# A decoder trunk on one core: the down projection as seven products over quadrants, with their sums made during the up projection, and three moves in the front

## The chip, the core and the metric

The kernel runs on one core of a Trainium2 chip. Five engines have instruction streams of their own: TensorE (PE in the profile) multiplies matrices into eight banks of PSUM, VectorE (DVE) and GpSimd (POOL) do elementwise work, ScalarE (ACT) does casts, copies and activations, and SyncE (SP) does little else than issue DMAs. An engine takes its instructions in order; engines wait for each other by semaphores. SP's, ACT's and POOL's DMA issues stand in the same in-order streams.

The metric is the device time of one execution in microseconds (us). A profiled execution also gives a span, from the first to the last instruction.

## What is computed

```python
h = rmsnorm(x, norm_mix_g)                    # x: 1024 tokens x 1024 features
z = h @ w_in                                  # a_h a_b a_c | q k v | c_val c_gate
y_a = a_b * causal_dwconv(a_c * a_h, conv_a_w)
y_b = dilated_mixture(q, k, v, rel_bias)      # 8 heads of 64
u = causal_dwconv(c_val * sigmoid(c_gate), conv_c_w) + conv_c_b
y_c = silu(layernorm(u, ln_c_g, ln_c_b))
y = concat(rmsnorm(y_a), rmsnorm(y_b), rmsnorm(y_c))
x = x + y @ w_out
h = rmsnorm(x, norm_ffn_g)
gate, val = split(causal_dwconv(h @ w_up, conv_f_w))   # 2 x 2816
x = x + (silu(gate) * val) @ w_down           # 2816 x 1024
return rmsnorm(x, final_g)
```

All is float32. The inner dimension of the down projection is 2816, which is 22 feature steps of 128.

## The kernel before

**Arithmetic.** PE works on a rounded format (fp32r). To keep the precision of float32, every operand is cut into a high part (a cast on ACT, helper line L71) and a low part (a subtraction on DVE or POOL, line L72), and every product is made of three matmuls (`mm3`, lines L90 to L92): high by high, and the two of high by low. A matmul here has a 128x128 stationary and a 128x512 moving operand.

**Order.** The order of PE's instructions is the order of the code. The other engines' and the DMA queues' instructions are put in order by a scheduler, which places each where its own model of the run finds it ready; so an instruction can come to stand ahead of one that is written earlier. Tiles come from pools with few buffers, and a tile that is used again makes its next writer wait for its last reader.

**Front (to 445 us).** The input projections come first. While they run, DVE makes the 31-tap convolution of the third part, `conv_rest`, whose two halves are added to `ln_a` (L432). Column sums for the norms are made on PE (`st_ps`, L116) at set places of a later projection: a hook is called after so many of its steps, by the table `HK`; a second hook fetches the result (`st_c` on DVE, `tr_ps` on PE). q and k for a pair of heads are projected (`proj_qk`), split, stored to DRAM, and read back by head as `sa`, `sb` and `sm` (`load_head`, POOL's queue). Attention starts at 231 us (`s_ps`, L527), and between its steps PE does fill work from a generator: the remaining q and k, then `out_ac`, the output projection of two of the three parts, which needs `w_out` as `wac_hi` and `wac_lo`.

**Up projection (529 to 929 us).** The 1024x1024 products of a step j (one gate and one value tile of 128 features) are made as seven products on quadrants. `main(j)` runs 22 times: POOL makes four sums of weights (L971 to L974), operands are split, PE fills banks `cb`, and DVE adds them up (L979, L983, L988, L997, L1000) into `ut`. A three-tap convolution follows (`conv3`, ACT and four DVE operations at L960), then silu, and the product of gate and value (L1006), which is stored to DRAM as `actd[j]` (L1007), 128 features by 1024 tokens. `lead` makes the first two of the seven products ahead of time; steps 6, 13, 20 and 21 have none, and are shorter.

**Down projection (929 to 1173 us).** For each half of the tokens, PE goes over 22 feature steps; a step takes a 128x1024 tile of `w_down` and a 128x512 tile of `actd` from DRAM, splits them, and adds to eight banks. The first two steps of the first half have tiles loaded and split during the up loop (`early_tiles`, into buffers of the up projection). A bank that is done is added to x (L1098), squared and summed (ACT), and `finish` scales and stores the output.

## Time and profile before

| | us |
|---|---|
| median of three runs | 1182.11 (1181.99 to 1182.67) |
| profiled run | 1181.71 |
| its span | 1179.9 |
| PE busy | 1138.5 (96%) |
| DVE busy | 757.4 (64%) |
| POOL busy | 521.3 (44%) |
| ACT busy | 503.7 (43%) |

The mean granted clock of PE is 0.984 of full speed. In the rows below, times are in us from the start of the span unless marked ns. A timeline row gives start and length of an instruction (or of several of one kind, x4), engine, code line, operation, output <- inputs, and in brackets how long the engine was idle before and what released it. The length of a matmul is the life of one instruction in a pipeline and not the distance to the next. "PE f_ps L90 <- ACT wac_hi L71" reads: the matmul at L90 that writes f_ps waited for the cast that writes wac_hi. In a row of windows each engine's busy time is followed by its count of instructions; PEclk is the granted clock, and the last two numbers are the busy share of the DMA engines and GB/s.

### The profile page before, as it was taken

Reading aid. Unit: us, or ns where it says so; the run is one execution under the profiler, and the core shown is the slowest. Engines: PE = TensorE matmul, PEld = TensorE weight load, DVE = VectorE, ACT = ScalarE, POOL = GpSimd, SP = SyncE. Lnnn points to the kernel's source line nnn. Section 1 sums busy time; section 2 is a strip of 40 time slices with the busy share of each in tenths; the row PEclk is TensorE's granted clock in tenths of the full one; section 3 lists DMA queues with packets and bytes.
Section 4 is the critical chain, followed back from the end, with each engine's and each line's share of the span. In section 5 each row is a group of like instructions: output and inputs, shape, how many; then the busy total and the mean of one; then the engine's idle time right before and its main releaser. Section 6 shows DMA issues by size and latency. Waiting matters only on the chain.

```text
span 1179.9 us, 14291 instructions
## 1 busy us (share of the span) xinstructions
PE 1138.5 (96%) x5327; PEld 943.7 (80%) x5327; DVE 757.4 (64%) x886; ACT 503.7 (43%) x798; POOL 521.3 (44%) x328
## 2 busy tenths in 40 slices
PE   9999979899979999989999999999999999999997
PEld 7888868788858887868888888888887788888886
DVE  7599965356656666796677887788778722164214
ACT  7212115256555655573444444444444432343323
POOL 4223522423222203036677777777776043334331
PEclk9999989999989999989999999999999999999999
DMA  6218214977689604223242342332423554456531
GB/s 239 86 40 234 73 53 121 309 195 166 156 236 228 143 1 161 96 102 124 78 138 89 108 141 83 133 108 90 142 89 126 169 191 158 146 188 217 171 116 72
DMA packets 59317, 162.80 MB, mean 138 GB/s; under 512 B 6232, under 2 KB 15952, under 8 KB 59248
## 3 DMA queue, kind: packets, MB, share of 16 engines
q1 hardware_dynamic: 44784, 139.27, 36.1%
q0 software_dynamic: 12160, 16.78, 7.2%
q10 hardware_dynamic: 2304, 5.83, 1.4%
q8 instruction: 42, 0.69, 0.3%
q14 instruction: 27, 0.22, 0.1%
HBM read 127.17 MB, written 34.69 MB: 137 GB/s over the span
## 4 chain that ended last, share of the span: by engine, by line
PE 83%; DVE 6%; DMA 5%; ACT 3%; issue 2%; POOL 1%; SPq 0%; ACTq 0%; DVEq 0%; POOLq 0%
PE cb L91 8%; PE cb L90 8%; PE cb L92 8%; PE d_ps L92 7%; PE d_ps L91 6%; PE d_ps L90 6%; PE ca L92 4%; PE ca L90 4%; PE ca L91 4%; PE pv_ps L581 2%; PE f_ps L90 2%; PE f_ps L92 2%; PE f_ps L91 2%; PE t_ps L550 2%; PE v L92 1%
## 5 line engine op out<-in xcount | busy, mean ns | idle before, releaser
L72 POOL TENSOR_TENSOR w_lo<-w_raw,w_hi 128x1024 fp32r<-128x1024 f32 (+2 forms) x49 | 108.7, 2220 | 204.6 <-ACT w_hi L71 204.6
L960 DVE SCALAR_TENSOR_TENSOR x<-ut,pr,x 128x1024 f32<-128x1024 f32 x88 | 147.0, 1688 | 18.8 <-ACT x L958 18.0
L72 POOL TENSOR_TENSOR wd_lo<-w_raw,wd_hi 128x1024 fp32r<-128x1024 f32 x32 | 78.4, 2454 | 163.3 <-ACT wd_hi L71 150.7
L92 PE MATMUL d_ps<-wd_hi,a_lo 128*128 128x512 f32 x336 | 131.7, 392 | 1.2 <-DVE a_lo L72 1.2
L90 PE MATMUL d_ps<-wd_hi,a_hi 128*128 128x512 f32 x336 | 131.5, 391 | 0.5 <-ACT a_hi L71 0.5
L91 PE MATMUL d_ps<-wd_lo,a_hi 128*128 128x512 f32 x336 | 131.4, 391 | 0.5 <-POOL wd_lo L72 0.5
L72 DVE TENSOR_TENSOR a_lo<-a_raw,a_hi 128x512 fp32r<-128x512 f32 x42 | 40.0, 961 | 132.4 <-ACT a_hi L71 125.3
L71 ACT CAST w_hi<-w_raw 128x512 fp32r<-128x512 f32 (+2 forms) x61 | 46.1, 764 | 138.8 <-PE v L92 23.6
L298 DVE SCALAR_TENSOR_TENSOR yc<-u,pr,yc 128x1024 f32<-128x1024 f32 x60 | 89.7, 1548 | 1.7 <-ACT yc L295 1.4
L92 PEld LDWEIGHTS d_ps<-wd_hi,a_lo 128*128 128x128 f32 x336 | 63.5, 189 | 14.6 <-DVE a_lo L72 1.5
L90 PEld LDWEIGHTS d_ps<-wd_hi,a_hi 128*128 128x128 f32 x336 | 63.5, 189 | 14.2 <-ACT a_hi L71 1.0
L91 PEld LDWEIGHTS d_ps<-wd_lo,a_hi 128*128 128x128 f32 x336 | 63.4, 189 | 13.9 <-POOL wd_lo L72 0.8
L71 ACT CAST a_hi<-a_raw 128x512 fp32r<-128x512 f32 x42 | 25.8, 620 | 111.9 <-PE d_ps L91 108.6
L958 ACT ACTIVATE x<-ut,pr 128x1024 f32<-128x1024 f32 x44 | 50.7, 1153 | 47.8 <-DVE ut L1000 32.6
L537 ACT ACTIVATE p<-p,mn 128x128 f32<-128x128 f32 (+3 forms) x64 | 49.8, 778 | 40.5 <-DVE mn L534 40.3
L1006 DVE TENSOR_TENSOR x<-x 128x1024 f32<-128x1024 f32 x22 | 46.3, 2105 | 10.6 <-ACT x L1005 10.6
L71 ACT CAST wd_hi<-w_raw 128x1024 fp32r<-128x1024 f32 x42 | 43.9, 1048 | 20.0 <-DMA w_raw<-in 20.0
L997 DVE TENSOR_TENSOR ut<-cb,yb 128x512 f32<-128x512 f32 x22 | 15.2, 690 | 56.3 <-PE cb L92 56.3
L561 DVE TENSOR_TENSOR ptl<-t_ps,pth 128x512 fp32r<-128x512 f32 x48 | 33.1, 690 | 20.6 <-ACT pth L560 20.1
L971 POOL TENSOR_TENSOR xp<-xp 128x512 f32<-128x512 f32 x11 | 21.2, 1925 | 55.2 <-DMA xp<-in 49.8
L550 PE MATMUL t_ps<-ident,p 128*128 128x128 f32 x288 | 44.4, 272 | 0.0
L534 DVE CUSTOM_DVE_ANT_0 p<-l_ps,g 128x640 f32<-128x640 f32 (+5 forms) x34 | 33.8, 995 | 15.0 <-PE l_ps L528 14.4
(405 smaller groups left out, 3319.1 us busy)
## 6 DMA issues: line engine op xcount, KB each, us to landing
w_raw<-in SPq DMA_DIRECT2D x93, 512.0 KB, 3.7
ur<-in SPq DMA_DIRECT2D x22, 512.0 KB, 3.7
xp<-in SPq DMA_DIRECT2D x22, 512.0 KB
actd<-x SPq DMA_DIRECT2D x22, 512.0 KB
a_raw<-actd SPq DMA_DIRECT2D x42, 256.0 KB, 2.8
vd<-vt SPq DMA_DIRECT2D x8, 512.0 KB
vv<-vd POOLq DMA_DIRECT2D x8, 512.0 KB, 5.4
g<-fs SPq DMA_DIRECT2D x8, 512.0 KB, 9.5
```

The lines of the kernel that those rows point to most:

```text
L71: cp = A.copy(hi, src)
L72: lo_eng.tensor_tensor(out=lo, in0=src, in1=f(hi), op=ALU.subtract)
L90: T.matmul(ps, whi, xhi, start=start, stop=False, **kw)
L91: T.matmul(ps, whi, xlo, start=False, stop=False, **kw)
L92: T.matmul(ps, wlo, xhi, start=False, stop=stop, **kw)
L298: V.scalar_tensor_tensor(out=yc[i], in0=u[i][:, j:j + S], scalar=col("cwc", j * 2 + i), in1=yc[i], op0=ALU.mult, op1=ALU.add)
L534: V.tensor_tensor_reduce(out=p[:, :n], in0=ps[:, :n], in1=gq, op0=ALU.add, op1=ALU.min, scale=1.0, scalar=3e38, accum_out=mn[:, ix:ix + 1])
L537: mark["exp"] = A.activation(out=p[:, :n], in_=p[:, :n], func=AF.Exp, scale=-1.0, bias=mn[:, ix:ix + 1], accum_out=den[h // 2][:, dc:dc + 1])
L550: T.transpose(out=tp[:, i * P:(i + 1) * P], in_=p[:, kj * P:(kj + 1) * P], identity=ident)
L958: A.activation(out=c, in_=t[:, 2:], func=AF.Copy, scale=col("cwf", 2 * 44 + m))
L960: V.scalar_tensor_tensor(out=c, in0=t[:, q:q + S], scalar=col("cwf", q * 44 + m), in1=c, op0=ALU.mult, op1=ALU.add)
L1006: V.tensor_tensor(out=cg, in0=cg, in1=cv, op=ALU.mult)
```

## The change

**Down projection.** It becomes seven products over quadrants, as the up projection is. The activation (2816 x 1024 tokens) is cut into A11, A21 (features of steps 0 to 10, first and second half of the tokens) and A12, A22 (steps 11 to 21), and `w_down` into B11, B12 (steps 0 to 10, first and second half of the output columns) and B21, B22 (steps 11 to 21). P1 is A11 B11, P2 is A12 B21, and five more products work on the sums S1, S2 (of the activation) and T1, T2, T3 (of the weights) too. Each product goes over eleven feature steps with four banks, one for each 128 tokens; there are two sets of four banks, d_x and d_y, and P2 and P3 add on to what P1 and P5 left. A step loads each operand as a quadrant of 128x512, and P7, P4 and P3 load a third quadrant and subtract it on POOL.

T1 and T2 are made during steps 0 to 10 of the up loop, S1 and S2 during steps 11 to 21, one DVE and one POOL operation a step: `sums_load(j)` reads into the buffers that the product of gate and value leaves free, `sums_add(j)` adds and stores the sums to DRAM. T3 is made during P1, P6 and P2 (`third`). The early tiles now cover four feature steps of P1. The three matmuls in a bank and step stay as they were.

**Front.** The table `HK` gets other places, q and k of the first pair of heads stay in SBUF, and their loads are issued ahead of the last projection; `out_ac` loads the first half of `w_out` into other buffers before it opens its own, splits it in two cuts, and loads x on SP's queue.

```diff
-    HK = (6, 8, 8, 10, 9, 11, 5, 9)
+    HK = (10, 14, 7, 11, 8, 12, 5, 9)
...
         split(t[:, :S], hi, lo, G if tmp else V)
+        if i % 4 == 0:
+            qk[i] = hi, lo
+            return
         nc.sync.dma_start(out=qk[i][0], in_=f(hi))
...
     do_norm()
+    heads = {0: load_head(0), 1: load_head(1)}
     table(AF.Exp, "sqrt")
     proj_qk(5, 10, (yb[2], yb[3].bitcast(F32R), yb[2].bitcast(F32R)))
...
-        mark["w"] = split(raw, hi, lo, G)
+        for q in range(2):
+            q = slice(q * 512, q * 512 + 512)
+            mark["w"] = split(raw[:, q], hi[:, q], lo[:, q], G)
...
     def out_ac():
 
+        w2 = [wp_pair() for _ in range(2)]
+        for q, r in enumerate((0, 6)):
+            load_half(r, 0, *w2[q])
         close(c_x)
...
+            if dh == 0:
                 for q in range(2):
-                    load_row(2 + q, *wac[q])
+                    nc.sync.dma_start(out=xp2[q], in_=x_n[q * P:(q + 1) * P, :])
+                for q, r in enumerate((0, 6)):
+                    load_half(r, 1, *wac[q])
...
+    def sums_load(j):
+
+        cg, cv = xp2[2 * (j % 2)], xp2[2 * (j % 2) + 1]
+        if j < HF:
+            nc.sync.dma_start(out=cv, in_=w_down[j * P:(j + 1) * P, :])
+            nc.sync.dma_start(out=cg[:, HS[1]], in_=w_down[(j + HF) * P:(j + HF + 1) * P, HS[1]])
+        else:
+            nc.sync.dma_start(out=cv, in_=actd[j - HF])
+
+    def sums_add(j):
+
+        cg, cv = xp2[2 * (j % 2)], xp2[2 * (j % 2) + 1]
+        x11, x12, x22 = cv[:, HS[0]], cv[:, HS[1]], cg[:, HS[1]]
+        if j < HF:
+            V.tensor_tensor(out=x11, in0=x12, in1=x11, op=ALU.subtract)
+            G.tensor_tensor(out=x22, in0=x22, in1=x11, op=ALU.subtract)
+            to = (("T1", j, x11), ("T2", j, x22))
+        else:
+            G.tensor_tensor(out=x12, in0=x12, in1=x22, op=ALU.add)
+            V.tensor_tensor(out=x11, in0=x12, in1=x11, op=ALU.subtract)
+            to = (("S1", j - HF, x12), ("S2", j - HF, x11))
+        for n, i, t in to:
+            nc.sync.dma_start(out=sums_d[n][i], in_=t)
...
         nc.sync.dma_start(out=actd[j], in_=cg)
+        sums_load(j)
+        if j:
+            sums_add(j - 1)
...
         if j in (FT - 3, FT - 2):
-            early[j - FT + 3] = early_tiles(j - FT + 3)
+            for q in range(2):
+                early[2 * (j - FT + 3) + q] = early_tiles(2 * (j - FT + 3) + q)
+    sums_add(FT - 1)
...
+    SRC = {"P1": ((A11,), (B11,)), "P6": ((S2,), (T2,)), "P2": ((A12,), (B21,)), "P7": ((A11, A21), (T3,)),
+           "P5": ((S1,), (T1,)), "P4": ((A22,), (T2, B21)), "P3": ((A12, S2), (B22,))}
...
+                x = dn.tile([P, 512], F32, name=f"{e}_raw{i}", tag=f"{e}_raw{i}", bufs=NBUF)
+                nc.sync.dma_start(out=x, in_=quadrant(spec, kt))
+                raws.append(x)
+            raw = raws[0]
+            if len(raws) > 1:
+                G.tensor_tensor(out=raw, in0=raw, in1=raws[1], op=ALU.subtract)
...
+            split(raw, hi, lo, V)
...
+    run("P1", "x", done1)
+    for t in range(8):
+        nc.sync.dma_start(out=x3[t], in_=x2d[t])
+    run("P6", "y", done6)
+    run("P2", "x", done2)
+    run("P7", "y", done7)
+    run("P5", "x", done5)
+    run("P4", "y", done4)
+    run("P3", "x", done3)
```

Three places of the order show what moved. DVE in the front, behind the sum `ln_a` (`st_c` is the first fetched statistic, `pd` and `ah` belong to the short convolution); first the kernel before:

```order
L432 TENSOR_TENSOR ln_a<-yc_112,yc_113 128x1024
L404 TENSOR_TENSOR ah<-ah,r1b 128x1024
L123 TENSOR_SCALAR st_c<-st_ps 128x8
L411 TENSOR_TENSOR pd<-ac,ah 128x1024
L139 COPY tr_r<-tr_ps 8x128
L414 SCALAR_TENSOR_TENSOR ah<-pd,pr,ah 128x1024 x2
```

and the changed kernel at the same place:

```order
L452 TENSOR_TENSOR ln_a<-yc_112,yc_113 128x1024
L424 TENSOR_TENSOR ah<-ah,r1b 128x1024
L431 TENSOR_TENSOR pd<-ac,ah 128x1024
L434 SCALAR_TENSOR_TENSOR ah<-pd,pr,ah 128x1024 x2
L123 TENSOR_SCALAR st_c<-st_ps 128x8
L139 COPY tr_r<-tr_ps 8x128
```

The fetch of the statistic stands behind `pd` and both operations on `ah` now. DVE in the up loop, from the product of gate and value of a step (L1006 before, L1056 after) to the first sums of the next; before:

```order
L1006 TENSOR_TENSOR x_2609<-x_2609 128x1024
L983 TENSOR_TENSOR yb_83<-cb,yb_83 128x512
L988 TENSOR_TENSOR ut_3693<-cb,yb_83 128x512
L72 TENSOR_TENSOR so_lo_3687<-ur_3689,so_hi_3685 128x512
L997 TENSOR_TENSOR ut_3693<-cb,yb_83 128x512
L72 TENSOR_TENSOR w_lo<-w_raw,w_hi 128x512
```

and after, in one of the later steps:

```order
L1056 TENSOR_TENSOR x_2621<-x_2621 128x1024
L1033 TENSOR_TENSOR yb_83<-cb,yb_83 128x512
L1038 TENSOR_TENSOR ut_3697<-cb,yb_83 128x512
L72 TENSOR_TENSOR so_lo_3691<-ur_3693,so_hi_3689 128x512
L977 TENSOR_TENSOR x_2621<-x_2621 128x512
L1047 TENSOR_TENSOR ut_3697<-cb,yb_83 128x512
L72 TENSOR_TENSOR w_lo<-w_raw,w_hi 128x512
```

The sum L977 stands between the last split and L1047, the L997 of before. SP's queue at the end of the up loop; before (L1007 is the store of a step's product, L1040 and L1045 load weights and activation of a down step, L1092 loads x):

```order
L1007 DMA actd_4136<-x_2609 128x1024
L1045 DMA a_raw<-actd_4118 128x512
L1045 DMA a_raw<-actd_4119 128x512
L1045 DMA a_raw<-actd_4120 128x512
L1045 DMA a_raw<-actd_4121 128x512
L1092 DMA x_0_7040<-x2d_3732 128x1024
L1007 DMA actd_4137<-x_2609 128x1024
L1092 DMA x_1_7041<-x2d_3733 128x1024
```

and after (L1057 is the store of the last product, L965 the reload for a sum, L980 the stores of sums, L1113 loads for T3, L1098 the loads of a down step):

```order
L1057 DMA actd_4141<-x_2621 128x1024
L965 DMA x_2621<-actd_4130 128x1024
L980 DMA S_4185<-x_2621 128x512
L980 DMA S_4196<-x_2621 128x512
L1140 DMA gfrow<-in 128x1024
L1113 DMA t_0_7274<-in 128x512
L1113 DMA t_1_7275<-in 128x512
L1113 DMA t_0_7316<-in 128x512
L1113 DMA t_1_7317<-in 128x512
L1098 DMA a_raw_7322<-actd_4124 128x512
L1098 DMA b_raw_7328<-in 128x512
```

Before, the tiles of the first down steps were asked for ahead of the last product's store; now the first of them, for feature step 4, stand behind the last sums and ten issues.

## Rows read from the trace of the kernel before

**Rows 1.** Windows of the up (560:880) and down projection (990:1130); the columns stand first.

```profile
core 0: us, PE busy (x) PEld busy (x) DVE busy (x) ACT busy (x) POOL busy (x), PEclk, DMA share, GB/s
...
560.00:880.00 320.00, 320.00 (x1414) 265.13 (x1413) 244.78 (x214) 143.79 (x203) 238.67 (x146) 1.00 0.33 110
...
990.00:1130.00 140.00, 140.00 (x619) 116.04 (x618) 46.17 (x55) 46.37 (x72) 49.22 (x20) 1.00 0.54 174
```

**Rows 2.** The page's costliest groups: one of the down projection's three matmul lines.

```profile
L92 PE MATMUL d_ps<-wd_hi,a_lo 128*128 128x512 f32 x336 | 131.7, 392 | 1.2 <-DVE a_lo L72 1.2
```

**Rows 3.** PE's waits over the whole span: total us, times, longest us.

```profile
PE st_ps L116 <- DVE ln_a L432: 7.2, 1, 7.2
...
PE f_ps L90 <- ACT wac_hi L71: 5.0, 1, 5.0
...
PE s_ps L527 <- DMA sm<-qk: 4.2, 1, 4.2
...
PE f_ps L91 <- POOL wac_lo L72: 1.6, 1, 1.6
```

**Rows 4.** Windows just after three of these waits; columns as in rows 1.

```profile
158.60:167.00 8.40, 8.36 (x28) 7.30 (x29) 2.43 (x3) 1.72 (x2) 3.60 (x2) 0.51 0.00 0
...
232.00:236.00 4.00, 4.00 (x14) 3.31 (x13) 1.22 (x5) 1.10 (x4) 0.96 (x1) 0.61 1.01 370
...
342.00:352.00 10.00, 6.43 (x20) 4.94 (x21) 0.67 (x1) 2.67 (x3) 5.65 (x3) 0.54 0.73 259
```

**Rows 5.** Timeline of DVE in one step of the up loop: start, length, work, idle before.

```profile
601.56 0.69 DVE L997 TENSOR_TENSOR ut<-cb,yb 128x512 f32<-128x512 f32 x1 [3.47 <-PE cb L92]
...
612.65 2.37 DVE L1006 TENSOR_TENSOR x<-x 128x1024 f32<-128x1024 f32 x1 [0.53 <-ACT x L1005]
...
620.60 0.69 DVE L997 TENSOR_TENSOR ut<-cb,yb 128x512 f32<-128x512 f32 x1 [3.59 <-PE cb L92]
```

**Rows 6.** Timelines of POOL and of SP's DMA queue in the same step.

```profile
601.62 1.30 POOL L974 TENSOR_TENSOR xp<-xp 128x512 f32<-128x512 f32 x1
...
615.04 0.33 SPq L1007 DMA_DIRECT2D actd<-x  x1
```

**Rows 7.** DMA issues by tile: KB of one, median us from issue to landing.

```profile
w_raw<-in SPq DMA_DIRECT2D x93, 512.0 KB, 3.7
...
a_raw<-actd SPq DMA_DIRECT2D x42, 256.0 KB, 2.8
```

**Rows 8.** Timeline of PE at the passage from the up to the down projection.

```profile
928.97 0.39 PE L90 MATMUL d_ps<-b11h 128*128 128x512 f32 x1
...
938.26 0.39 PE L92 MATMUL d_ps<-b21h,b21l 128*128 128x512 f32 x1
...
941.87 0.80 PE L92 MATMUL d_ps<-wd_hi,a_lo 128*128 128x512 f32 x1 [1.19 <-DVE a_lo L72]
```

**Rows 9.** Timelines of DVE and ACT at the same passage.

```profile
935.25 1.23 DVE L1006 TENSOR_TENSOR x<-x 128x1024 f32<-128x1024 f32 x1 [1.13 <-ACT x L1005]
...
938.53 2.17 ACT L71 CAST a_hi<-a_raw 128x512 fp32r<-128x512 f32 x4
```

**Rows 10.** Timelines of POOL and DVE at the start of the down projection.

```profile
947.63 4.76 POOL L72 TENSOR_TENSOR wd_lo<-w_raw,wd_hi 128x1024 fp32r<-128x1024 f32 x2 [7.50 <-ACT wd_hi L71]
...
950.49 2.45 DVE L72 TENSOR_TENSOR a_lo<-a_raw,a_hi 128x512 fp32r<-128x512 f32 x1 [6.87 <-ACT a_hi L71]
...
955.93 0.69 DVE L72 TENSOR_TENSOR a_lo<-a_raw,a_hi 128x512 fp32r<-128x512 f32 x1 [2.99 <-ACT a_hi L71]
```

**Rows 11.** Windows with high traffic in the front: columns as in rows 1.

```profile
8.00:18.00 10.00, 9.86 (x44) 7.83 (x43) 8.06 (x6) 9.25 (x11) 4.09 (x3) 1.00 1.03 398
...
204.00:212.00 8.00, 8.00 (x37) 6.60 (x36) 5.25 (x5) 2.11 (x2) 4.51 (x5) 1.00 1.16 310
```

**Rows 12.** Timeline of PE at the end: the last matmul.

```profile
1172.68 0.39 PE L92 MATMUL d_ps<-wd_hi,a_lo 128*128 128x512 f32 x1
```

**Rows 13.** Timeline of DVE in the front: the sum ln_a.

```profile
157.28 1.22 DVE L432 TENSOR_TENSOR ln_a<-yc,yc 128x1024 f32<-128x1024 f32 x1
```

More of the change, by code (lines that the diff above doesn't have):

```diff
@@ L911, in body @@
     actd = [dr.tile([P, S], F32, name=f"actd{j}") for j in range(FT)]
+    HF = FT // 2
+    sums_d = {n: [dr.tile([P, 512], F32, name=f"{n}{i}") for i in range(HF)] for n in ("T1", "T2", "T3", "S1", "S2")}
     LEAD = 4
@@ L1032, in body @@
     xo = [dn.tile([P, D], F32, name="xo", tag="xo", bufs=2) for _ in range(2)]
[L1033 to L1049 removed]
+    x3 = [dn.tile([P, D], F32, name=f"x3_{t}") for t in range(8)]
@@ new lines, in third, with square @@
+    def third(i):
+        x = [dn.tile([P, 512], F32, name=f"t3_{n}", tag=f"t3_{n}", bufs=2) for n in range(2)]
+        for t, spec in zip(x, (B22, B12)):
+            nc.sync.dma_start(out=t, in_=quadrant(spec, i))
+        G.tensor_tensor(out=x[0], in0=x[0], in1=x[1], op=ALU.subtract)
+        nc.sync.dma_start(out=sums_d["T3"][i], in_=x[0])
+    def square(t, dh):
+        q = HS[dh]
+        A.activation(out=xo[t % 2][:, q], in_=x3[t][:, q], func=AF.Square,
+                     accum_out=s3[:, 2 * t + dh:2 * t + dh + 1])
@@ L1058, in finish @@
         V.reciprocal(out=r, in_=r)
-        for q in HS if last else (slice(0, D),):
-            if last and q == HS[0]:
+        for q in HS if last is not None else (slice(0, D),):
+            if last is not None and q == HS[0]:
                 A.activation(out=x[:, q], in_=last[:, q], func=AF.Copy, scale=r)
@@ new lines, in body, with dmm @@
+    nc.sync.dma_start(out=gfrow, in_=grow[1:2, :].broadcast_to([P, D]))
+    banks = {}
+    def dmm(n, y, t, kt, ops, start=True):
+        if (n, t) not in banks:
+            banks[n, t] = dps.tile([P, 512], F32, name=f"d_{y}{t}", tag=f"d_{y}{t}") if start else banks[start_of[n], t]
+        ah, al, bh, bl = ops
+        ts = slice(t * P, (t + 1) * P)
+        mm3(banks[n, t], ah[:, ts], al[:, ts], bh, bl, start and kt == 0, kt == HF - 1,
+            **({} if start else {"skip_group_check": True}))
@@ new lines, in body, with run @@
+    extra = {"P1": 0, "P6": 4, "P2": 8}
+    start_of = {"P2": "P1", "P3": "P5"}
+    def run(n, y, done):
+        lag = LAG if n == "P3" else 1
+        tiles = {}
+        for kt in range(HF):
+            if n in extra and kt % 3 == 1 and extra[n] + kt // 3 < HF:
+                third(extra[n] + kt // 3)
+            ops = tiles[kt] = early[kt] if n == "P1" and kt in early else down_tiles(n, kt)
+            if kt < HF - lag:
+                for t in range(4):
+                    dmm(n, y, t, kt, ops, n not in start_of)
+        for t in range(4):
+            for kt in range(HF - lag, HF):
+                dmm(n, y, t, kt, tiles[kt], n not in start_of)
+            done(t, banks[n, t])
@@ new lines, in tt, with done1, done6, done2 @@
+    def tt(o, a, b, op=ALU.add, eng=V):
+        eng.tensor_tensor(out=o, in0=a, in1=b, op=op)
+    def done1(t, ps):
+        A.copy(p1[t], ps)
+    def done6(t, ps):
+        tt(u2[t], ps, p1[t])
+    def done2(t, ps):
+        tt(x3[t][:, HS[0]], ps, x3[t][:, HS[0]])
+        square(t, 0)
+        tt(x3[t][:, HS[1]], x3[t][:, HS[1]], u2[t])
+    def done7(t, ps):
+        tt(u3[t], ps, u2[t])
+        x = x3[4 + t]
+        for q in HS:
+            tt(x[:, q], x[:, q], u3[t])
+    def done5(t, ps):
+        tt(x3[4 + t][:, HS[1]], ps, x3[4 + t][:, HS[1]])
+        square(4 + t, 1)
```

148 lines of the change are left out of this document (64 added, 84 removed).

## The prediction

> **What bounds the kernel now.** I read the windows of the trace first, because the change takes matmuls away. TensorE (PE) is the bound. In the up projection PE is busy 320.00 of 320 us at full clock, in the down projection 140.00 of 140, while VectorE (DVE) and GpSimd (POOL) are near three quarters busy in the one and a third in the other [rows 1]. A matmul of these shapes costs its pitch, not its record: 320.00 us hold 1414 matmuls and 140 us hold 619, so one costs 0.2263 and 0.2262 us [rows 1]. The record says 392 ns [rows 2], because it overlaps the next; with it every sum below would come out 1.7 times too large. I use 0.2266 us.
>
> Second, the list of PE's waits: four large ones stand ahead of the up projection, 7.2 us for ln_a, 5.0 and 1.6 us for the wac weights and 4.2 us for sm [rows 3]. Behind each the granted clock falls to the lower of its two levels for a while: 0.51 in the 8.4 us after the first, 0.61 in the 4 us after sm, 0.54 in the 10 us after wac [rows 4]. A wait thus costs more than its length.
>
> Third, what the other engines do where the change puts its work: DVE and POOL in one step of the up loop, and every queue at the passage from up to down.
>
> **The down projection, part by part.** Before, 2 halves x 22 feature steps x 8 banks x 3 passes are 1056 matmuls; after, 7 products x 11 steps x 4 banks x 3 are 924. All have one shape, so 132 x 0.2266 = **29.9 us** leave PE. That is the gain if nothing else becomes late. What becomes late:
>
> *The up loop.* Each of 22 steps gets two sums of 512 columns, one on DVE and one on POOL, two or one loads and two stores. A 512-column DVE operation is 0.69 us and a POOL one 1.30 us [rows 5, 6]. DVE is busy 244.78 and POOL 238.67 of 320 us [rows 1]; in a step of 19.04 us DVE waits 3.59 us for PE ahead of L997 [rows 5]. So the busy time alone fits. What can fail to fit is the new chain. The sum of a step uses the buffer that the gate product (L1006) frees: product, store of actd, reload of the same buffer, sum; and the sum stands in DVE's order ahead of the next step's L1047 (the old L997). From the start of L997 (601.56) to the end of L1006 (615.02) is 13.46 us [rows 5]. Two issues of 0.33 us [rows 6], a landing of 3.7 us for 512 KB [rows 7] and the sum of 0.69 us give 18.5 us: inside 19.04. From step 11 on POOL's sum of 1.30 us comes first: 19.8 us, 0.75 us too long. The order has it ahead of L1047 in five of the steps from 11 on and right behind it in two more; six times 0.75 make a slip of DVE of about **4.5 us** (bounds 0, if stores land faster, and 12, twice the excess in every step). PE does not feel that at once, since its products have several banks ahead; I let it appear at the passage.
>
> *The passage from up to down.* Before, the first down matmul starts at 928.97, right behind the last up product; two early feature steps carry PE to 938.49, then it waits three times, 1.19 us the longest [rows 8]. After, four early steps of 12 matmuls carry it 48 x 0.2266 = 10.9 us. The next operands must be there by then, and they are queued late. SP issues in order; after the store of the last product it has the reload of an old actd tile, two stores that wait for the sums, gfrow, four loads for the third sum, and only then the loads of feature step 4. Before, the last product ended at 936.48 [rows 9], 7.5 us after the first down matmul; with the slip, 12.0. Behind it: store and reload issues 0.66, landing 3.7, POOL 1.30, DVE 0.69, six issues (the second store, gfrow, four loads) 2.0, the two loads of step 4 0.66 and 2.8 to land [rows 7], the ScalarE cast 0.6 [rows 9] and the split 0.69 [rows 10]: 13.1 us, and 1 us for passing semaphores (my allowance: the idle time behind a releaser is 0.5 us ahead of L1006 [rows 5]). PE goes on 26.1 us after the first down matmul instead of 10.9: **a gap near 15 us**, and 2 us at the lower clock (an estimate from 1.7 us lost behind the present waits; bounds 1 and 3). This eats half of the gain.
>
> *The rest of the stage.* 73 steps x 12 x 0.2266 = 198.5 us. P7, P4 and P3 add a POOL subtraction a step (1.30 of 2.72 us) and two splits on DVE (1.4 of 2.72): they fit, at the price above. Loads of 187 quadrants, the third sums, x and the output are about 64 MB in 209 us, 306 GB/s, where before moved 174 [rows 1]. The trace has stretches at 398 and at 310 GB/s [rows 11], so I count it as just hidden, with 4 us where eight x tiles are queued between P1 and P6 (bounds 0 and 8). POOL's and DVE's extra finishing in P4 and P3: 1.5 us. From the end of the last matmul's pitch (1172.68 + 0.23) to the end of the span it is 7.0 us before [rows 12]; after, four blocks end 2.04 us apart (9 matmuls) and each needs about 2.4 us of DVE, so 1.5 us more: 8.5.
>
> Sum from the first down matmul: 26.1 + 2 + 198.5 + 4 + 1.5 + 8.5 = **240.6 us**, against 1179.9 - 929.0 = 250.9 before: **-10.3 us**.
>
> **The front.** (A) The statistics matmuls move back by 4 and 6 steps of a projection. The 7.2 us wait [rows 3] ends when DVE finishes ln_a at 158.5 [rows 13]; moved work covers it all but about 1.8 us. But st_c now stands behind pd and two more operations in DVE's order, so the later statistics wait (1.75, 2.3 and 4.6 us by my walk through the order). Net -3.5 us (0 to -7). (B) Heads 0 and 4 of q and k no longer go through DRAM ahead of the loads of sa, sb, sm: the 4.2 us and 1 us of lower clock behind it, -5.2 us (0 to -5.5). (C) The first w_out halves are loaded early, the split is cut in two: 5.0 + 1.6 us [rows 3] and 2.8 us of lower clock, less up to 3 us because a load of yd now stands behind eight x loads on SP: -6.5 us (-3 to -9.4). Together **-15.2 us** (-8 to -20).
>
> All in all -25.5: a span of 1154.4, a run of 1156.2 (the profiled run has 1.8 us outside its span), and 1156.6 beside a median that is 0.4 above the profiled run. **I predict 1157.**
>
> **A rule against it.** Where DVE reads two operands from SBUF while POOL works, one of them waits: the a_lo split of 128x512 took 2.45 us while POOL split a weight tile over 947.63 to 952.39, and 0.69 us when POOL was idle [rows 10]. The new sum on DVE and every split of the down stage are of just that kind. The Trainium skill, page "SBUF — State Buffer", section "Who interferes with whom", says that the pair of ports is a lock held for a whole instruction, so that such work adds up and does not overlap; the rows agree. By that rule the up loop gets a price, which is the first rival.
>
> **Rivals.**
> R1, *the two engines add up*. In a step POOL's 8.5 operations x 1.25 and DVE's two-input operations, 7.45 us, take turns: 18.1 of 19.04 us. The change adds 0.60 + 1.25: 19.95, so 0.9 us a step in 18 long steps, 16 us, less the slip already counted (2): 1157 + 14 = **1171**. For it: rows 10. Against: 18.1 is worked out from medians, and POOL still has idle time in a step.
> R2, *transfers bound the down stage*. If rows of 2 KB move at 282 GB/s (my reading of a mixed stretch), 64 MB need 227 us, not 209, and the 4 us of stalls are in that: 1157 + 14 = **1171**. For it: 306 GB/s asked is close to the 310 of one of the rows 11, and every load waits in one queue. Against: 398 GB/s in the other.
> R3, *nothing waits*. The slip and the gap vanish because the loads land earlier, or POOL and DVE sit free: 29.9 less 5 for the clock and the tail, and 20 at the front: 1182 - 45 = **1137**.
> R4, *slower*: the up loop becomes bound by its chain through DRAM. If DVE's loop (13.46 us, store, reload, two sums) takes over 20.5 us, the excess is paid 22 times on PE: 21.0 us make 22 x 1.95 = 43 us, less the 25.5 of the forecast and the slip: about **1196**. It decides from 1.47 us a step on. For it: L1006 took 2.37 us in one step [rows 5] and a reload may queue behind weight loads. Against: two thirds of the steps have 0.5 us of room by the rows.
> R5, *the front gives nothing*, as its waits come back at the next statistics and the next load: **1170**.
>
> **How the numbers follow.** Forecast 0.59, R1 0.10, R2 0.09, R3 0.08, R4 0.08, R5 0.06. Of the forecast's own spread (slip 0 to 12, stalls 0 to 8, front -8 to -20) come -14 and +18 us: 1143 to 1175; R1, R2 and R5 lie inside. R3 and R4 stay out, 0.16. A measurement of this kernel tells about 0.2%, 2.4 us, from no change. Faster by more: forecast, R3 and nearly all of R1, R2, R5: 0.88. Within: 0.04 (R1 or R2 at twice its price). Slower: 0.08.
>
> **What would show it.** Right: 924 matmuls in the down stage at a pitch of 0.2266; a PE wait of 10 to 18 us soon after the last up product, released by a split of a quadrant; no wait over 2 us at ln_a, sm and wac. The slip: L1047 waits for L977 and not for PE from step 11 on. Wrong: PE waits inside the up loop (R1, R4), or P2 to P3 at more than 2.8 us a step with PE waiting for casts that wait for loads (R2). If P1's step 4 begins without a wait, the SP argument fails, and the time falls toward R3.

## The result, and the profile after

The changed kernel takes **1231.19 us** (1230.1 to 1234.23) where the kernel before takes 1182.05 beside it: a ratio of 1.042, interval 1.0399 to 1.0442. The forecast was 1157. The change is slower by 49 us, and the mechanism of the rival R4, which I gave 0.08, is the largest part of it. One execution of e14 below took 2243.96 us, almost twice its other three; it is in no figure here, and nothing on record explains it.

The page of the changed kernel: span and instructions, busy time and share of each engine, and the granted clock in 40 slices.

```profile
span 1228.4 us, 14932 instructions
...
PE 1132.0 (92%) x5195; PEld 928.6 (76%) x5195; DVE 854.5 (70%) x1026; ACT 519.0 (42%) x872; POOL 538.5 (44%) x366
...
PEclk9999987999999999899999899999899878999998
```

There are 132 matmuls fewer, but PE's busy time falls by only 6.5 us, in part since matmuls at the lower clock last longer (the mean granted clock is 0.958, before 0.984), and 84 us of the span are waits of 0.4 us or more, before 31. A ledger from four marks of the two traces (start of the last `pv_ps` matmul, which closes attention; end of the first and of the last product of gate and value, L1006 before and L1056 after; end of the span):

| stretch | before, us | after, us | difference | forecast |
|---|---|---|---|---|
| to the end of attention | 447.6 | 445.0 | -2.6 | -15.2 |
| to the first product of gate and value | 109.9 | 114.4 | +4.5 | 0 |
| first to last product of gate and value | 379.0 | 429.8 | **+50.8** | +4.5 |
| last product to the end | 243.4 | 239.1 | -4.3 | -14.8 |

The ledger compares one execution of each. Seven traces have this front (the changed kernel, e1, e2, e4, e5, e9, e10), and attention ends in them between 445.0 and 453.4 us, so the -2.6 of the first row is within their spread; the third row is far outside it.

The waits of PE after (compare [rows 3]; total us, times, longest):

```profile
PE d_x L90 <- ACT b_hi L71: 15.2, 1, 15.2
PE cb L90 <- DVE ut L1038: 15.1, 10, 3.4
PE st_ps L116 <- DVE ss_a L378: 13.3, 2, 12.8
PE cb L856 <- DVE b22l L72: 8.9, 1, 8.9
...
PE d_y L90 <- ACT b_hi L71: 3.7, 1, 3.7
...
PE d_x L91 <- DVE b_lo L72: 3.1, 1, 3.1
```

The three waits of [rows 3] for wac and sm are gone and that for ln_a is 1.8 us, as forecast. Two others stand in the front in their place (ss_a, b22l). 15.2 us is the gap at the passage, which I had put at 15. The second row is the up loop. Its windows, with the down stage's (columns as in [rows 1]):

```profile
560.00:880.00 320.00, 300.17 (x1273) 243.47 (x1272) 232.34 (x207) 121.20 (x179) 233.06 (x146) 0.97 0.48 160
1006.60:1010.40 3.80, 3.80 (x8) 2.76 (x9) 3.77 (x6) 3.05 (x5) 0.00 (x0) 0.50 1.05 394
1031.60:1037.70 6.10, 6.10 (x14) 4.50 (x15) 2.78 (x5) 2.47 (x4) 0.00 (x0) 0.50 1.06 383
1040.00:1195.00 155.00, 155.00 (x685) 128.24 (x684) 116.24 (x160) 75.14 (x145) 54.14 (x37) 1.00 0.81 272
```

In 320 us of the up loop PE gets through 1273 matmuls, not 1414 [rows 1]. DVE (232 us) and POOL (233 us) are no busier than before (245 and 239): neither is full. They wait for each other, so the step has become a chain. DVE's two longest waits from 560 to 960 us are both for what the sums need, in 8 and 11 of the steps, where before DVE waited for PE [rows 5]:

```profile
DVE x L977 <- POOL x L976: 41.8, 8, 7.5
DVE x L972 <- DMA x<-in: 40.5, 11, 4.0
```

From 1040 to 1195 the down stage runs without a gap at 0.2263 us a matmul, the pitch of before.

**The chain of an early step**, on DVE and SP's queue (start, length, work, idle before and releaser; L1016 is a weight load of the up projection, L962 the reload, L972 the sum):

```profile
618.90 2.36 DVE L1056 TENSOR_TENSOR x<-x 128x1024 f32<-128x1024 f32 x1 [0.53 <-ACT x L1055]
...
627.13 1.55 DVE L972 TENSOR_TENSOR x<-x 128x512 f32<-128x512 f32 x1 [3.87 <-DMA x<-in]
628.61 0.68 DVE L1047 TENSOR_TENSOR ut<-cb,yb 128x512 f32<-128x512 f32 x1
...
639.96 2.33 DVE L1056 TENSOR_TENSOR x<-x 128x1024 f32<-128x1024 f32 x1 [0.52 <-ACT x L1055]
```

```profile
620.21 0.33 SPq L1016 DMA_DIRECT2D ur<-in  x1
621.29 0.33 SPq L1057 DMA_DIRECT2D actd<-x  x1
621.67 0.43 SPq L962 DMA_DIRECT2D x<-in  x1
```

The product ends at 621.26. Its store goes out at 621.29, the reload at 621.67; the reload is there at 627.1, **5.5 us** after its issue and not 3.7. Two transfers of the same size, 512 KB, are ahead of it: the store, and the weight load of 620.21. The weight load makes more of the difference than the store. In the two early steps that issue no weight load so late, with the store alone ahead, the reload is there about 4.1 us after its issue; one of them issues it at 683.33 and has its sum at

```profile
687.50 0.69 DVE L972 TENSOR_TENSOR x<-x 128x512 f32<-128x512 f32 x1 [2.90 <-DMA x<-in]
```

The sum at 627.13 takes 1.55 us and not 0.69. L1047 starts 7.35 us after the product's end, and the next product ends 13.7 us later (13.46 in [rows 5]): 21.0 us, where I had 18.5 and PE needs 19.04.

**A late step**, on DVE and on POOL:

```profile
889.13 2.37 DVE L1056 TENSOR_TENSOR x<-x 128x1024 f32<-128x1024 f32 x1 [0.53 <-ACT x L1055]
...
899.43 1.76 DVE L977 TENSOR_TENSOR x<-x 128x512 f32<-128x512 f32 x1 [5.94 <-POOL x L976]
901.11 0.68 DVE L1047 TENSOR_TENSOR ut<-cb,yb 128x512 f32<-128x512 f32 x1
...
911.22 2.37 DVE L1056 TENSOR_TENSOR x<-x 128x1024 f32<-128x1024 f32 x1 [0.53 <-ACT x L1055]
```

```profile
894.13 1.29 POOL L1022 TENSOR_TENSOR xp<-xp,xp 128x512 f32<-128x512 f32 x1 [1.49 <-DMA xp<-in]
...
896.87 1.29 POOL L1024 TENSOR_TENSOR xp<-xp 128x512 f32<-128x512 f32 x1
898.11 1.28 POOL L976 TENSOR_TENSOR x<-x 128x512 f32<-128x512 f32 x1
```

The reload is issued at 891.89, 0.4 us after the product's end (891.50), again behind a weight load and the store. From 897.0 us on the DMA engines are idle, so its data have moved by then:

```profile
897.00:899.40 2.40, 2.40 (x12) 2.01 (x11) 0.00 (x0) 0.00 (x0) 2.40 (x3) 1.00 0.01 3
```

POOL's sum stands behind three weight sums of the next step and starts at 898.11, about 1 us after the data. It takes 1.28 us and DVE's sum behind it 1.76. So L1047 starts 9.6 us after the product's end; the rest takes 12.5 us here, and the step 22.1 us, where I had 19.8.

**The passage**, on PE and on SP's queue (compare [rows 8]):

```profile
980.32 0.39 PE L90 MATMUL d_x<-b11h 128*128 128x512 f32 x1
...
1006.60 0.80 PE L90 MATMUL d_x<-b_hi,a_hi 128*128 128x512 f32 x1 [15.23 <-ACT b_hi L71]
```

```profile
995.32 1.05 SPq L980 DMA_DIRECT2D S<-x  x2
996.59 0.33 SPq L1140 DMA_DIRECT2D gfrow<-in  x1
996.97 1.87 SPq L1113 DMA_DIRECT2D t<-in  x4
998.88 0.43 SPq L1098 DMA_DIRECT2D a_raw<-actd  x1
```

PE goes on 26.3 us after its first down matmul; the sum had said 26.1. The queue order is as drawn there: sums' stores, gfrow, four loads, and then the first operand (nine issues from the last product's store on, not ten). But the first operand, issued at 998.88, is there only 6.4 us later, when the cast of it starts, and in that time the DMA engines are full:

```profile
1005.25 0.62 ACT L71 CAST a_hi<-a_raw 128x512 fp32r<-128x512 f32 x1 [15.74 <-DMA a_raw<-actd]
```

```profile
999.00:1006.60 7.60, 0.00 (x1) 0.00 (x1) 0.69 (x1) 1.29 (x3) 2.53 (x2) 0.50 0.99 334
```

### The profile page after: what moved, and what is told of

Read it like the earlier page. It is cut to its first block, busy times and chain, and to the rows that moved or that the text cites. A ratio compares the mean times of both kernels' runs of the same rounds, so it can differ in the third digit from the quotient of the medians.

```text
span 1228.4 us, 14932 instructions
## 1 busy us (share of the span) xinstructions
PE 1132.0 (92%) x5195; PEld 928.6 (76%) x5195; DVE 854.5 (70%) x1026; ACT 519.0 (42%) x872; POOL 538.5 (44%) x366
## 5 line engine op out<-in xcount | busy, mean ns | idle before, releaser
L72 POOL TENSOR_TENSOR w_lo<-w_raw,w_hi 128x512 fp32r<-128x512 f32 (+2 forms) x51 | 108.9, 2140 | 190.9 <-ACT w_hi L71 190.9
L1008 ACT ACTIVATE x<-ut,pr 128x1024 f32<-128x1024 f32 x44 | 50.8, 1153 | 156.8 <-DVE ut L1047 87.5
L90 PE MATMUL d_x<-b_hi,a_hi 128*128 128x512 f32 x160 | 63.6, 398 | 15.2 <-ACT b_hi L71 15.2
L72 DVE TENSOR_TENSOR b_lo<-b_raw,b_hi 128x512 fp32r<-128x512 f32 x73 | 61.6, 843 | 10.5 <-ACT b_hi L71 10.2
L91 PE MATMUL d_x<-b_lo,a_hi 128*128 128x512 f32 x160 | 64.1, 400 | 3.3 <-DVE b_lo L72 3.1
L92 PE MATMUL d_x<-b_hi,a_lo 128*128 128x512 f32 x160 | 63.4, 396 | 0.0
L90 PE MATMUL d_y<-b_hi,a_hi 128*128 128x512 f32 x132 | 52.7, 400 | 3.7 <-ACT b_hi L71 3.7
L91 PE MATMUL d_y<-b_lo,a_hi 128*128 128x512 f32 x132 | 52.6, 398 | 0.0
L92 PE MATMUL d_y<-b_hi,a_lo 128*128 128x512 f32 x132 | 52.3, 396 | 0.0
L71 ACT CAST b_hi<-b_raw 128x512 fp32r<-128x512 f32 x73 | 45.1, 618 | 14.0 <-POOL b_raw L1102 6.1
L1056 DVE TENSOR_TENSOR x<-x 128x1024 f32<-128x1024 f32 x22 | 42.9, 1951 | 10.5 <-ACT x L1055 10.5
L977 DVE TENSOR_TENSOR x<-x 128x512 f32<-128x512 f32 x11 | 16.2, 1473 | 47.9 <-POOL x L976 47.9
L90 PEld LDWEIGHTS d_x<-b_hi,a_hi 128*128 128x128 f32 x160 | 30.8, 193 | 22.2 <-ACT b_hi L71 15.7
```

What stands on the lines that cost most here:

```text
L71: cp = A.copy(hi, src)
L72: lo_eng.tensor_tensor(out=lo, in0=src, in1=f(hi), op=ALU.subtract)
L90: T.matmul(ps, whi, xhi, start=start, stop=False, **kw)
L91: T.matmul(ps, whi, xlo, start=False, stop=False, **kw)
L92: T.matmul(ps, wlo, xhi, start=False, stop=stop, **kw)
L1008: A.activation(out=c, in_=t[:, 2:], func=AF.Copy, scale=col("cwf", 2 * 44 + m))
```

## Experiments

Every ratio is against the kernel before, run beside it on the same chip (medians 1182.6 to 1183.1 us). Runs e1 to e4, e5 to e8, e9 to e12 and e13 to e15 were each made on a chip of their own.

**Take the sums' work out of the up loop.** The kernel leaves out reloads and sums; the stores stay and write halves of the product in the sums' place.

```diff
-        sums_load(j)
-        if j:
-            sums_add(j - 1)
+        for n, q in (("T1", 0), ("T2", 1)) if j < HF else (("S1", 0), ("S2", 1)):
+            nc.sync.dma_start(out=sums_d[n][j % HF], in_=cg[:, HS[q]])
...
-    sums_add(FT - 1)
```

> The changed kernel with the reloads and the additions for T1, T2, S1 and S2 left out of the up loop; the two stores of each step stay (they store halves of the step's product), so P6, P5, P4, P3 work on other numbers. Theory 1 (the sums' chain through DRAM bounds the up loop): the step goes back from 20.8 us (first eleven) and 22.2 us (later) to 19.05 us, 50 us less, and since nothing waits for sums at the passage, the wait there falls from 15.2 to about 5 us: 1168 us (1163 to 1175). Rival 2 (stores and the stores' place in SP's order hold back weight loads): the step stays above 20 us and the time above 1200. Rival 3 (the down stage itself, with 306 GB/s, costs what the products save): the up loop recovers but the down stage from its first matmul to the end stays at 246 to 248 us even without the wait: 1180.

Measured: 1180.12 us, ratio 0.9972 (0.996 to 0.9985); from the first to the last product of gate and value 382.5 us. The window of its up loop is that of before again, 1414 matmuls:

```profile
560.00:880.00 320.00, 320.00 (x1414) 264.96 (x1413) 242.44 (x217) 142.96 (x202) 234.14 (x144) 1.00 0.41 142
```

The loop is 47 us shorter, and 3.5 us longer than in the kernel before (379.0). So stores and their traffic cost 3.5 us at most, and reload and sums 47 us. That fits theory 1, but this run takes out their chain, their traffic and their work together; the next runs keep the work. 12 us are missing to the expected 1168: the wait at the passage was 9.0 us and not 5, and the down stage took 244.5 us from its first matmul to the end. That is rival 3 in part (246 to 248 us even without a wait), and the last experiments are about it.

**Move the sum off the chain, leave the work.** With `mark["mult"]` on the product:

```diff
-            sums_add(j - 1)
+            with tc.issue_after(mark["mult"].ins):
+                sums_add(j - 1)
```

> The changed kernel with one order added: DVE's sum of step j-1 stands right behind the product of gate and value of step j, one step after its reload was issued, and not ahead of the first addition of step j. All work stays. Theory 1 (the chain: product, store, reload, sum, first addition of the next step): no DVE wait for the reload is left, the step falls to 19.05 to 19.4 us, and the time to 1180 (1176 to 1190). Rival 2 (DVE and POOL add up on SBUF operands, 18.1 + 1.85 us a step): the step falls only to 19.9 to 20.2 us, 1231 - 51 + 20 = 1200 (1195 to 1208). If neither chain nor ports are the cause, the time stays at 1225 or more.

Measured: 1215.0 us, ratio 1.026 (1.0237 to 1.0282), 412.1 us for the loop: 17.7 of 47 us went. Neither number that I gave for theory 1 or for rival 2 came. DVE's waits in the up loop tell why:

```profile
DVE x L1010 <- ACT x L1008: 43.5, 17, 4.5
DVE ut L1047 <- PE cb L92: 20.5, 11, 4.1
```

The first wait, at most 1.2 us a step in the kernel before, is 2.6: the convolution writes the buffer from which the late sum is still being stored (ACT's L1008 waits ten times for a store of T or S). One wait had taken the other's place. So the sums were given a tile of their own.

```diff
+        o1, o2 = xp2[7][:, HS[0]], xp2[7][:, HS[1]]
...
-            V.tensor_tensor(out=x11, in0=x12, in1=x11, op=ALU.subtract)
-            G.tensor_tensor(out=x22, in0=x22, in1=x11, op=ALU.subtract)
+            V.tensor_tensor(out=o1, in0=x12, in1=x11, op=ALU.subtract)
+            G.tensor_tensor(out=o2, in0=x22, in1=o1, op=ALU.subtract)
```

> The changed kernel with the late sum of the run before this one and, besides, both sums written to a tile that is free in this stage (the second half of the x tiles), so that the next convolution need not wait until the sums' stores have landed. Theory 1 (the 2.6 us that DVE waits for the convolution's first ScalarE operation behind the late sum come from that store): this wait goes back to 1.2 us, the step falls from 19.8 to 19.1 us (first eleven) and below 19.5 (later), the time to 1190 (1184 to 1197). Rival 2 (DVE and POOL add up to 19.9 us a step): it stays at 19.7 us or more a step, 1208 or more.

Measured: 1208.27 us, ratio 1.0226 (1.0191 to 1.0261), 405.0 us. The convolution's wait is 16.8 us in 17 again, and the first ten steps take 18.93 us each (18.62 without sums, e1): there theory 1 holds. The nine after them take 20.7 (18.9 in e1). In those, SP's queue waits, and POOL too (from 810 to 965 us; L1023 is a weight sum):

```profile
SPq L981 <- POOL xp L977: 69.5, 8, 12.4
```

```profile
POOL xp L1023 <- DMA xp<-in: 9.2, 3, 3.4
```

The store of S1 waits up to 12.4 us for POOL's sum, and the weight load that POOL's own next sums need stands behind it in SP's order (store at 847.09 us, load at 847.50). POOL waits for SP and SP for POOL.

**Free the operands too.** Reload into tiles that are free in the up loop, ahead of the product; both sums on DVE behind it.

```diff
     def main(j):
+        sums_load(j)
...
-            nc.sync.dma_start(out=cv, in_=actd[j - HF])
+            nc.sync.dma_start(out=xp2[7], in_=actd[j - HF])
...
-            G.tensor_tensor(out=x12, in0=x12, in1=x22, op=ALU.add)
+            V.tensor_tensor(out=x12, in0=x12, in1=x22, op=ALU.add)
...
+        with tc.issue_after(mark["mult"].ins):
+            sums_add(j, cg)
```

> The changed kernel with the operands of the sums in x tiles that are free during the up loop, loaded ahead of the product of gate and value, and both sums of a step on DVE right behind that product; POOL has none. The reload no longer waits for the product, and POOL's order and SP's stores that wait for POOL are out of it. Theory 1 (chain, POOL's place and SP's order made 20 of the 47 us each in the later runs): from the first to the last product of gate and value 383 to 390 us as without sums (382.5), not 429.8 (changed kernel) or 405.0 (late sums in their own tile); the time 1182 to 1190. Rival 2 (work on SBUF operands by DVE and POOL adds up; 1.2 us a step of it is left): 405 us again, 1205.

Measured: 1188.9 us, ratio 1.0048 (1.0033 to 1.0064), 392.8 us for the loop: 37 of the 47 us are gone, with the same sums, loads and stores. Theory 1 had said 383 to 390 us, rival 2 405. The run moves three things at once (the reload's place, POOL's sum, SP's order), so it does not tell what each of them is worth. The window of the loop and one sum:

```profile
560.00:880.00 320.00, 316.70 (x1388) 260.93 (x1387) 289.62 (x246) 139.49 (x199) 247.87 (x141) 0.99 0.51 172
```

```profile
635.28 1.79 DVE L971 TENSOR_TENSOR xp<-xp 128x512 f32<-128x512 f32 x1
```

DVE is busy 290 of 320 us now. In the window of e1 it has 29 operations fewer; at 0.69 us each they would add 20 us, and its busy time is 47 us more. A sum that is 0.69 us alone takes 1.79 beside POOL, as in [rows 10]: it starts at 635.28 and ends at 637.07, 0.56 us after a split of POOL (635.17 to 636.51). The row agrees with the Trainium skill, "SBUF — State Buffer", section "Who interferes with whom": a DVE instruction with two SBUF inputs contends with a GpSimd instruction that reads SBUF, and the port pair that they share is an exclusive lock. So R1 exists. That it makes the 10 us which are left (392.8 against 382.5) is argued and not tested; in any case it is not what made the change slower.

**The front, apart and whole.** e3 and e4 are the change's two halves as the diff has them; e7 and e8 are the pieces of it on `load_head` with `qk[i]` and on `out_ac` with `load_half`; e12 is e7 and e8 together. e6 is one line:

```diff
-    HK = (6, 8, 8, 10, 9, 11, 5, 9)
+    HK = (10, 14, 7, 11, 8, 12, 5, 9)
```

> The kernel before with the down projection of the change (sums, early tiles, seven products) and none of its front. In the traces the front of the change starts attention's end 2.6 us earlier and then loses 4.5 us up to the first product of gate and value. If the front is as good as neutral, 1229 to 1231 us; if the 4.5 us belong to the front's other order, 1229; if they belong to the sums, 1234.

> The kernel before with the front edits alone (table of places, heads 0 and 4 kept in SBUF and loaded early, first halves of the output weights early). Theory 1 (the gain of three removed waits is given back by one new wait of 12.8 us for the second sum of squares and 17 us at the lower clock): attention ends 2.6 us earlier, 1179.5 us (1177 to 1181). Rival (the loss of 4.5 us in the transposing stage that follows is the front's too): 1184. My forecast's 15 us: 1167.

> The kernel before with the new table of places for the column sums and nothing else. Theory 1 (the 12.8 us wait for the second sum of squares needs the early head loads, whose traffic holds back the row of the layer norm): the ln_a wait of 7.2 us falls to 1.8 and no wait over 4 us takes its place: 1179 (1176 to 1181). Rival (the table alone makes the fetch of the row too late: it stood 6.7 us later): a wait of 5 to 9 us at the second sum of squares, 1183 to 1186.

> The kernel before with q and k of the first pairs of heads kept in SBUF and their head loads issued ahead of the last projection, nothing else. If their traffic alone holds back rows that are fetched through DRAM, a new wait of 3 us or more shows in the norms and the time stays near before's, 0 to +3. If not: the wait of 4.2 us for sm and 1 us of lower clock go, -5 us.

> The kernel before with the early and halved load of the first output weights and x on SP's queue, nothing else. In the run with all front edits the waits for these weights were gone but the later transposing stage had one wait of 8.9 us (b22l) instead of two of 4.1 in all, with the lower clock 3.4 us longer. If that wait is the cost of this edit: 5.0 + 1.6 + 2.8 gained, 5 + 1.7 lost, -2 to -3 us. If it comes from the head or the table edits: -6 to -9 us.

> The kernel before with the front edits but the table of places. Alone the heads gave -0.3% and the output weights -0.2%, the table +0.45%, all three together +0.3%. If they add up: -0.45 to -0.5%, 5 to 6 us less than before. If heads and weights pay for the same 4 us wait in the transposing stage: -2 to -3 us.

| edits on the kernel before | us | ratio (interval) |
|---|---|---|
| down projection alone (e3) | 1229.92 | 1.0401 (1.0379 to 1.0422) |
| front alone (e4) | 1186.46 | 1.003 (1.0015 to 1.0044) |
| table of places alone (e6) | 1187.97 | 1.0045 (1.003 to 1.006) |
| heads alone (e7) | 1179.97 | 0.9973 (0.996 to 0.9986) |
| output weights alone (e8) | 1180.75 | 0.998 (0.9966 to 0.9993) |
| heads and weights (e12) | 1180.19 | 0.9981 (0.9969 to 0.9994) |

The front as a whole loses 0.3% on the kernel before (the rival of e4, and 2 us more than it said). With the new down projection its cost isn't clear of noise: 1.042 with it, 1.0401 without (e3), and the intervals overlap. The table is the loss (the rival of e6, and 2 us more than it said; theory 1 there had 1179). With it alone the second sum of squares makes PE wait:

```profile
PE st_ps L116 <- DVE ss_a L378: 10.5, 2, 9.1
```

In the changed kernel this is 12.8 us; DVE and SP's queue there:

```profile
204.43 2.48 DVE L476 SCALAR_TENSOR_TENSOR yc<-yc,pr,ln_r 128x1024 f32<-128x1024 f32 x2 [14.11 <-DMA ln_r<-scr]
...
210.81 1.23 DVE L378 TENSOR_TENSOR ss_a<-ss_a,ss_s 128x1024 f32<-128x1024 f32 x1 [2.76 <-ACT ss_s L377]
```

```profile
190.15 0.65 SPq L142 DMA_DIRECT2D scr<-tr_r  x2
195.67 0.35 SPq L146 DMA_DIRECT2D ln_r<-scr  x1
```

The row of the layer norm goes to DRAM as `scr` and is read back as a tile of 512 KB. The new table has its store at 190 us (183 before). There the loads of the first head, eight of 256 KB on POOL's queue from 188.8 us on, are under way, and the way to DRAM and back takes 14 us. Before it took 5.3. The windows of the two ways, before and after:

```profile
183.00:188.50 5.50, 5.50 (x33) 4.75 (x31) 0.28 (x1) 0.82 (x1) 0.00 (x0) 1.00 0.50 176
```

```profile
190.00:204.50 14.50, 9.32 (x42) 7.37 (x40) 0.39 (x3) 0.00 (x0) 3.03 (x6) 0.89 1.16 251
```

With the table alone (e6) the row meets the head loads too, though they are issued later there (from 193.9 us). Heads and weights did less than forecast: -3 us and -2 us, not -5.2 and -6.5, and together not more (the rival of e12). e7 lies between its two cases: a new wait of 3.5 us shows and 3 us are gained. With the early weights, alone too, the transposing stage ahead of the up loop waits 7.8 to 8.9 us for b22l. The stretch from attention to the first product is 111.6 to 114.4 us in the twelve traces with these weights and 109.6 to 110.1 in the five without: that is the +4.5 us of the ledger.

**The passage and the products.** On top of e9, the queue ahead of P1 is cleared (e10), the old table comes back (e11), the x loads are spread (e13, with gfrow and the second operands of P7, P4 and P3 put behind the loads of their step), the output scalings are spread (e14), and the early weights are undone (e15). Here `mark["ld"]` is the last load of the step and `mark["sp"]` its last split:

```diff
-    nc.sync.dma_start(out=gfrow, in_=grow[1:2, :].broadcast_to([P, D]))
...
-    extra = {"P1": 0, "P6": 4, "P2": 8}
+    extra = {("P1", 6): 0, ("P1", 8): 1, ("P1", 10): 2}
+    extra.update({(n, kt): b + kt // 3 for n, b in (("P6", 3), ("P2", 7)) for kt in (1, 4, 7, 10)})
...
+            if n in ("P2", "P7") and kt in (2, 4, 6, 8):
+                t = (kt - 2) // 2 + (4 if n == "P7" else 0)
+                with tc.issue_after(mark["ld"].ins):
+                    nc.sync.dma_start(out=x3[t], in_=x2d[t])
...
-        finish(4 + t, None)
...
+            if n == "P3" and kt in (2, 4, 6, 8):
+                with tc.issue_after(mark["sp"].ins):
+                    finish(4 + (kt - 2) // 2, None)
```

> The run before this one with SP's queue cleared at the passage: the load of gfrow behind P1, and the eleven third sums moved back (three late in P1, four in P6, four in P2), so that the loads of P1's step 4 stand directly behind the last sums' stores. By my sum the wait falls by seven issues of 0.33 us and by what their 2.3 MB took: from 15 us (or what e9 shows) to 5 to 7 us, and the lower clock behind it from 10 to 3 us: 8 to 10 us less than e9. If the loads' landing and not their place makes the wait: less than 3 us.

> The run before this one with the table of places of the kernel before; the early heads and the early output weights stay. If the table alone costs what it did by itself (+5 us on the kernel before): 5 us less than e10, 1166 to 1174, faster than both kernels. If the early heads hold back the row of the layer norm whatever the table says: no change against e10.

> The kernel of e11 with the eight loads of x, the load of gfrow and the second operands of P7, P4 and P3 put in SP's order behind the loads of the feature step at which they stand (x one every second step in P2 and P7), and not in a block between P1 and P6. If that block makes the wait at the start of P6 (5.2 us in e11, 3.7 us in the changed kernel, with 6 us at the lower clock behind it): the wait falls below 1 us, 6 to 8 us less than e11. If the third sums and the rate of 2 KB rows make it: the wait stays above 3 us, less than 3 us gained.

> e13 with the four output scalings of the second token half each put behind the splits of a later feature step of P3 on DVE (steps 2, 4, 6, 8), and not in a block of 6.9 us (changed kernel) at the start of P3. If the block makes the wait at the start of P3 (3.1 us in the changed kernel, 5.4 in three parts in e11): no wait over 1 us there, 4 to 6 us less than e13. If the subtractions on POOL and their loads make it: less than 2 us.

> e14 with the first output weights loaded as in the kernel before; of the front only the early heads are left. The early weights gave -0.2% by themselves, and the early heads -0.3%, both together -0.2%: if the wait of 8.9 us for b22l that comes with the early weights eats all they gain, this run is 0 to 2 us faster than e14; if they gain on top, it is 2 to 4 us slower.

| kernel | us | ratio (interval) | first down matmul to the end, us |
|---|---|---|---|
| e9 | 1188.9 | 1.0048 (1.0033 to 1.0064) | 243.0 |
| e10 | 1189.48 | 1.0059 (1.0037 to 1.008) | 241.6 |
| e11 | 1180.5 | 0.9977 (0.9964 to 0.9991) | 244.9 |
| e13 | 1166.37 | 0.9851 (0.981 to 0.9892) | 229.3 |
| e14 | **1165.29** | **0.984** (0.9812 to 0.9869) | 226.9 |
| e15 | 1169.14 | 0.9879 (0.9851 to 0.9907) | 226.5 |

e10 missed: the wait at the passage fell from 8.8 to 4.4 us, but that at P6 rose from 3.7 to 6.0, and nothing was won. P1 only came sooner to the same block of loads (e13 bears that out). e11 gained 9 us on e10, more than the table cost by itself, but as e10 had gained nothing it stayed short of the expected 1174. e13 takes the block away, and the waits of e11

```profile
PE d_x L90 <- ACT b_hi L71: 7.8, 2, 5.3
...
PE d_y L90 <- ACT b_hi L71: 5.2, 1, 5.2
```

become, in e14,

```profile
PE d_x L90 <- ACT b_hi L1105: 4.2, 1, 4.2
...
PE d_x L91 <- DVE b_lo L1106: 1.9, 3, 1.4
```

with no wait for d_y. e13 brought 14 us, twice what was expected, since with the waits stretches at the lower clock went too (24 us at 0.50 behind the first down matmul in e11, 12 in e13). Between e13 and e14 the intervals overlap, so no gain in time is shown; in the one trace of each the stage is 2.4 us shorter and the wait at P3 falls from 2.2 us to 1.9 in three parts, 1.4 the longest, which is less than expected: the block of scalings, 6.9 us long in the changed kernel, was a part of that wait at most. (The 5.4 us in three parts, given above for e11, are e10's; e11 had 3.0 in two.) The block reads in the changed kernel:

```profile
1192.31 6.92 DVE L1134 SCALAR_TENSOR_TENSOR x<-x,s,gfrow 128x1024 f32<-128x1024 f32 x4
```

e15 against e14 leaves open whether the early weights gain: the intervals overlap. Loads do not bound the stage as a whole: from 990 to 1130 us of e14 PE never waits, at more traffic than the forecast asked for:

```profile
990.00:1130.00 140.00, 140.00 (x620) 115.91 (x619) 103.46 (x139) 65.34 (x128) 50.41 (x36) 1.00 0.90 311
```

e14 has the seven products, the early heads and the early weights, without the new table and with the sums off the chain. It is 1.6% faster than the kernel before, 18 us (1165.29 against 1183.07), and about 66 us faster than the changed kernel, which ran on another chip.

## Why the prediction was wrong

The miss is 74 us (1157 forecast, 1231 measured). By the ledger 46 us of it are the up loop, 17 the front up to the first product, and 10.5 the stretch behind the last product.

**The up loop, the step that failed.** I saw the chain (product, store, reload, sum, L1047) and priced it at 18.5 and 19.8 us. It measured 21.0 and 22.1. Three terms were too small. The reload's landing was priced at 3.7 us, the median of weight loads of that size [rows 7]; it was 5.5, since the weight load of the step and the product's store were both ahead of it, and 4.1 with the store alone. DVE's sum was priced at 0.69 us, though my own rule against the change said that it would meet POOL, and was 1.55 to 1.76. POOL's sum was priced at its length alone, 1.30 us, and waits about 1 us more in POOL's order. Together they make the step about 2.4 us longer than I had it. Then I made the excess a slip that shows once, at the passage. A loop that is longer than PE's step does that only until the banks ahead are used up; after that PE pays it every time. R4 had the mechanism, the price (1.95 us a step, 43 us) and the point of decision, and its chance was the error. e1 and e9 show it: the time comes back when the chain goes, with the same stores (e1), and 37 of 47 us of it with the same sums (e9).

**The passage: the sum came out, by luck.** 26.1 us forecast, 26.3 measured; 2 us at the lower clock forecast, 1.9 measured (3.8 us at 0.50). The queue that I drew is the one that ran, but two of the terms are wrong by 3 us each and cancel. The last product ended 8.9 us after the first down matmul, not 12.0, since the slip was paid in the loop and did not show here; and the first operand took 6.4 us from its issue, not 3.5 (0.66 and 2.8), as the DMA engines were full.

**The rest of the down stage: mechanisms right, sizes small.** The x block was 3.7 us of wait as forecast (4), but 6.1 us at the lower clock behind it cost 3 more; P4 and P3 cost 3.1 and 1.7, not 1.5; the tail measured 8.6 (8.5). From the first down matmul: 248.1 us, not 240.6. The waits of 15.2, 3.7 and 3.1 us each had a stretch at 0.50 behind them, and I had priced that only for the first.

**R1 and R2.** R1 (the engines add up) is real; 10 us of the 47 is the most that e9 leaves for it. R2 (transfers) falls as a price on the whole stage: 311 GB/s in e14, and 272 in the changed kernel from 1040 us on, without a wait. For a few us it is right: at the passage and behind P6's start the DMA engines are full (0.99 and 1.06 of their time) at 334 and 383 GB/s.

**The front.** I forecast -15.2 (bounds -8 and -20) and got +3.5 (e4); this step failed too. (A) ln_a's wait fell to 1.8 as forecast; the waits that I had walked through the order (1.75, 2.3 and 4.6 us) were one of 9 to 13, because I gave the row's way through DRAM the time it had before, and its new place met the loads of the first head. (B) and (C) removed the waits named, and gave 3 and 2 us: with the early heads a wait of 3.5 us for a statistic appears, with the early weights one of 7.8 for b22l.

**Slips in the sums.** The 187 quadrants are all 77 steps; without the early tiles the stage loads 179, which asks for 2 MB less. R2's 282 GB/s is named after no row, and R5 adds up to 1172. The 2.37 us of L1006, which I gave as a sign for R4, is its usual length and was in the 13.46 already. None of them would have moved the forecast.

## What to carry to other kernels

Where a change puts a store, a reload and a use of one buffer into a loop, write the loop down as a cycle over every queue in it, with the landing time behind every transfer that is issued just ahead of it and with what stands ahead on each engine; if it is longer than the bound engine's step, its excess is paid at each pass. Give such work its own buffers and issue the load a step ahead before anything else. A block of loads between two stages is worth spreading over the steps of the next: here that was 14 us of 1180, while spreading the finishing work showed no gain clear of noise. And check a sum by its terms: at the passage two errors of 3 us hid each other.
